# Last layer's feed-forward: GpSimd's scaling and adding given to VectorE and ScalarE, half of u's fp32 values by ScalarE, gates read a step apart

## The chip, the cores and the metric

One core of a Trainium2 chip runs the whole kernel. The metric is device time in microseconds (us); a kernel's number is the median of its runs. TensorE (PE) does matrix products and transposes, VectorE (DVE), ScalarE (ACT) and GpSimd (POOL) the elementwise work, and SyncE (SP) issues the transfers. Each engine runs its instructions in the order in which the program lists them.

## The reference

A backbone of two layers works on 256 latent and 256 context tokens of width 1024, batch 1. Layer 0 mixes by windowed attention, layer 1 (the last) by a state-space scan; each is followed by a feed-forward block of width 4096. Shifts, scales and gates (six vectors per layer) come from a small conditioning product with `w_mod`. What matters here, for the latent tokens `x` of the last layer:

```python
ALPHA = (2.0 * DEPTH) ** 0.25
def layer_norm(x, g, b):
    ...
    y = (xf - mu) * lax.rsqrt(var + LN_EPS) * g + b
def modulate(h, shift, scale):
    return h * (1.0 + scale) + shift
def squared_relu_mlp(h, w1, w2):
    return jnp.square(jax.nn.relu(h @ w1)) @ w2
```

The mixer's output, times its gate, is added to ALPHA times the stream and normalised (`mixg`, `mixb` are that norm's g and b). The result, modulated, goes through the feed-forward; the feed-forward's output, times its gate, is added to ALPHA times the same result and normalised again.

## The kernel before

All values are fp32. For TensorE each operand is split into a high part, rounded to fp32r, and a low part, the fp32 value less the high part; a product then takes three matmuls: high by high (L79), low by high (L80), high by low (L81). In the last layer the down-projections do the same on L261 to L263. PE is the busiest engine.

Weights stream from memory in 1 MB pieces named `raw` (`emit_w`, two buffers). ScalarE makes each high part `wh` (L61) and VectorE each low part `wl` (L62), 128x512 at a time. `next_w` hands out the next 1024 columns and emits pieces up to `ahead` further than the one asked for.

**Layer 0's feed-forward** runs in four rounds. In a round eight hidden blocks m0 to m7 are made (tile `f0a`): ScalarE does relu and square, VectorE squares again in fp32 (L357) and subtracts (L358), which gives the low part `f0fl`. Then eight output blocks (`f0b`) each need all eight hidden blocks, and VectorE adds each to the stream (L346). Between these steps the program draws single steps from a generator, `mods_sums`, that makes the last layer's modulation vectors. It loads eight 512 KB pieces `wm` (two buffers, so a piece is issued when the piece two before it has been used) and VectorE sums them, scaled, into `ma` (L140 the first, L142 the others, 128x1024 each). For the two gates (numbers 2 and 5) two matmuls on PE (L149) and two additions on VectorE (L150) follow, matmul and addition in the same step.

**The last layer's tail** works on rows: two tiles of 128 tokens, i = 0 and 1. For each tile the last part of the mixer's down-projection `so` ends on PE; the stream is transposed on PE and copied to `Xt` by ScalarE (L1021); VectorE multiplies by the gate, adds and takes statistics (L270 to L272, 128x512 each); L278 to L280 finish mean and deviation; L290 normalises the row tile in place. PE transposes it in 128x128 pieces (L296), two banks of four pieces. From each piece come

```python
nc.scalar.activation(uh[k][:, c], p, AF.Identity, bias=sh, scale=sc)
t = self.tmp.tile([128, 256], F32, tag="t1", name="ut")[:, :128]
nc.vector.tensor_scalar(t, p, sc, sh, op0=ALU.mult, op1=ALU.add)
nc.vector.tensor_sub(ul[k][:, c], t, uh[k][:, c].bitcast(F32))
```

which are L301 (`u4h`, ScalarE), L303 (`ut`, VectorE) and L304 (`u4l`, VectorE). The first four hidden blocks are made by rows: 24 matmuls per tile (`f1r`, L1034 to L1036), relu by ScalarE (L364, tile `rr`), square by VectorE (L365), four transposes on PE (L368), then high and low parts (L372, L373). From then on PE runs hidden blocks (`f1a`) and down-projections to the end.

The feed-forward's residual needs the normalised row tile times ALPHA g plus ALPHA b. GpSimd does that: `mixg` and `mixb` (128x1024, loaded by `row`) are scaled once (L1056), then each row tile is multiplied (L1058) and added to (L1059) in place, 128x1024 per instruction. The code stands behind round c = 0 of the last feed-forward; a scheduler places each instruction on its engine by priority and readiness, and GpSimd has nothing else to do by then.

Of the kernel before, what the change touches and what calls it, by code (L numbers as in the profile page):

```python
# [8 lines left out]
F32 = mybir.dt.float32  # L9
F32R = mybir.dt.float32r  # L10
BF16 = mybir.dt.bfloat16
AF = mybir.ActivationFunctionType
ALU = mybir.AluOpType
# [26 lines left out]
class Net:  # L40
# [90 lines left out]
    def mods_sums(self, i, b, streams, gate=None):  # L131
# [12 lines left out]
        if gate is not None:  # L144
            nc.sync.dma_start(gate, self.a["rows"][(2, 5).index(b), :].partition_broadcast(128))
            for h in range(2):
                c = slice(512 * h, 512 * h + 512)
                ps = self.bank("md", f"mod{i}{b}{h}")
                nc.tensor.matmul(ps, self.avg, acc[0][:, c], start=True, stop=True)  # L149
                nc.vector.scalar_tensor_tensor(gate[:, c], ps, 32.0 * 1024, gate[:, c], op0=ALU.mult, op1=ALU.add)  # L150
                yield
            return
# [133 lines left out]
    def ln_mid(self, i, x, st, aff, uh, ul):  # L286
# [5 lines left out]
        for q in range(2):  # L292
# [4 lines left out]
            for m in range(4):  # L297
                k = 4 * q + m
                p = pt[:, 128 * m:128 * m + 128]
                sc, sh = aff[:, 0, k:k + 1], aff[:, 1, k:k + 1]  # L300
                nc.scalar.activation(uh[k][:, c], p, AF.Identity, bias=sh, scale=sc)  # L301
                t = self.tmp.tile([128, 256], F32, tag="t1", name="ut")[:, :128]
                nc.vector.tensor_scalar(t, p, sc, sh, op0=ALU.mult, op1=ALU.add)  # L303
                nc.vector.tensor_sub(ul[k][:, c], t, uh[k][:, c].bitcast(F32))  # L304
# [666 lines left out]
    def layer1(self):  # L971
# [35 lines left out]
        with tc.tile_pool(name="tk", bufs=1) as self.tk, tc.tile_pool(name="fp1", bufs=2) as fp:  # L1007
            X = self.tk.tile([128, 2, 1024], F32, name="Xt")
            ws = [self.next_w(whole=True) for _ in range(4)]
            bn = [self.stat_tile(f"bm{i}") for i in range(2)]  # L1010
# [30 lines left out]
            for c in range(4):  # L1041
# [10 lines left out]
                for m in range(8 if c < 3 else 4):  # L1052
                    self.down(acc, lh(m), ll(m), self.next_w(whole=True), 8 * c + m, False)
                if c == 0:
                    for t in (ag, ab):
                        nc.gpsimd.tensor_scalar(t, t, ALPHA, 0.0, op0=ALU.mult, op1=ALU.add)  # L1056
                    for i in range(2):
                        nc.gpsimd.tensor_tensor(X[:, i, :], X[:, i, :], ag, op=ALU.mult)  # L1058
                        nc.gpsimd.tensor_tensor(X[:, i, :], X[:, i, :], ab, op=ALU.add)  # L1059
            ws = [self.next_w(whole=True) for _ in range(4)]  # L1060
# [106 lines left out]
```

## Time and profile before

| | us |
|---|---|
| runs of the kernel before | 1215.44, 1210.81, 1210.56 (median 1210.81) |
| the profiled execution | 1204.13 |
| its span | 1202.3 |
| PE busy | 1139.5 (95%) |
| VectorE busy | 845.2 (70%) |
| ScalarE busy | 600.7 (50%) |
| GpSimd busy | 62.7 (5%) |

The span runs from the first to the last instruction of the profiled execution; its granted TensorE clock was 0.984 of full speed on average. PE is busy nearly throughout, so the time is PE's work plus the few stretches in which PE waits or runs at the lower clock. The timelines list an engine's instructions by start, with the idle time ahead of one in brackets and what ended it; the chain of waits follows the end of the program back through what released each step.

### The profile page before, as it was taken

The page shows a single profiled execution, that of the slowest core. Times are in us where ns is not written, and L with a number is a line of the kernel's source. Part 1 is how long each engine was busy: PE and PEld are TensorE (multiplying, and loading weights), DVE is VectorE, ACT ScalarE, POOL GpSimd, SP SyncE. Part 2 cuts the span into 40 slices and gives each one's busy share as a digit, 9 for nine tenths or more (in the row PEclk, how much of TensorE's full clock was granted, in tenths as well). Part 3 has the DMA queues.
Part 4 walks back from the last instruction along what each step waited for, and adds up shares of the span by engine and source line. Part 5 has one row for each costly group of instructions (what it writes and reads, how often), then busy time and mean ns, then how long its engine had stood idle before and what let it go on. Part 6 is the DMA issues. An engine that isn't in the chain of part 4 may idle for free.

```text
span 1202.3 us, 18548 instructions
## 1 busy us (share of the span) xinstructions
PE 1139.5 (95%) x6976; PEld 916.9 (76%) x6976; DVE 845.2 (70%) x1701; ACT 600.7 (50%) x1372; POOL 62.7 (5%) x85
## 2 busy tenths in 40 slices
PE   5999999998999999989999898999999985999996
PEld 4766767887988878868898786777777674898995
DVE  4498677668958677744434889989898678565666
ACT  4376666235512322312323747787968654454551
POOL 1200000005000000000000500000000021000000
PEclk8999999999999999999999999999999997999999
DMA  8735331441645567633222125434544561555551
GB/s 327 296 109 172 110 125 48 136 145 38 206 144 179 167 215 277 222 131 105 93 82 72 44 108 160 141 116 166 171 144 143 215 220 47 188 185 180 197 186 70
DMA packets 41433, 182.79 MB, mean 152 GB/s; under 512 B 4608, under 2 KB 5248, under 8 KB 28288
## 3 DMA queue, kind: packets, MB, share of 16 engines
q1 hardware_dynamic: 41056, 181.36, 44.5%
q8 instruction: 55, 0.90, 0.3%
q10 hardware_dynamic: 288, 0.26, 0.1%
q14 instruction: 34, 0.28, 0.1%
HBM read 180.41 MB, written 1.18 MB: 151 GB/s over the span
## 4 chain that ended last, share of the span: by engine, by line
PE 77%; DVE 11%; DMA 5%; ACT 5%; issue 2%; DVEq 0%; SPq 0%; ACTq 0%
PE f0b L79 5%; PE f0b L81 5%; PE f0b L80 5%; PE f0a L79 5%; PE f0a L80 4%; PE f0a L81 4%; PE y L942 3%; PE o L503 2%; PE f L263 2%; PE f L262 2%; PE f1a L79 2%; PE f1a L81 2%; PE f1a L80 2%; PE f L261 2%; DMA wm<-in_w_mod 2%
## 5 line engine op out<-in xcount | busy, mean ns | idle before, releaser
L61 ACT CAST wh<-raw 128x512 fp32r<-128x512 f32 x404 | 237.4, 619 | 406.5 <-PE f0b L80 126.4
L62 DVE TENSOR_TENSOR wl<-raw,wh 128x512 fp32r<-128x512 f32 x404 | 268.9, 687 | 124.7 <-ACT wh L61 124.0
L80 PE MATMUL f0b<-f0fl,wh 128*128 128x512 f32 (+1 forms) x320 | 111.9, 350 | 3.5 <-DVE f0fl L358 3.5
L79 PE MATMUL f0b<-f0fh,wh 128*128 128x512 f32 (+1 forms) x320 | 114.6, 359 | 0.0
L79 PE MATMUL f0a<-u1h,wh 128*128 128x512 f32 (+1 forms) x320 | 111.4, 350 | 1.5 <-ACT u1h L181 1.5
L81 PE MATMUL f0b<-f0fh,wl 128*128 128x512 f32 (+1 forms) x320 | 112.3, 351 | 0.0
L81 PE MATMUL f0a<-u1h,wl 128*128 128x512 f32 (+1 forms) x320 | 110.9, 347 | 0.0
L80 PE MATMUL f0a<-u1l,wh 128*128 128x512 f32 (+1 forms) x320 | 110.9, 349 | 0.0
L142 DVE SCALAR_TENSOR_TENSOR ma<-wm,cs,ma 128x1024 f32<-128x1024 f32 x70 | 88.7, 1281 | 25.9 <-DMA wm<-in_w_mod 25.7
L80 PEld LDWEIGHTS f0b<-f0fl,wh 128*128 128x128 f32 x320 | 60.5, 189 | 13.6 <-DVE f0fl L358 4.2
L79 PEld LDWEIGHTS f0a<-u1h,wh 128*128 128x128 f32 x320 | 60.3, 189 | 11.7 <-ACT u1h L181 2.3
L81 PEld LDWEIGHTS f0b<-f0fh,wl 128*128 128x128 f32 x320 | 60.6, 189 | 10.5 <-issue 2.1
L79 PEld LDWEIGHTS f0b<-f0fh,wh 128*128 128x128 f32 x320 | 60.4, 189 | 10.6 <-issue 2.6
L81 PEld LDWEIGHTS f0a<-u1h,wl 128*128 128x128 f32 x320 | 60.6, 189 | 8.1 <-issue 0.4
L80 PEld LDWEIGHTS f0a<-u1l,wh 128*128 128x128 f32 x320 | 60.3, 189 | 7.8 <-issue 0.4
L79 PE MATMUL f1a<-u4h,wh 128*128 128x256 f32 x224 | 64.3, 287 | 0.0
L81 PE MATMUL f1a<-u4h,wl 128*128 128x256 f32 x224 | 64.1, 286 | 0.0
L80 PE MATMUL f1a<-u4l,wh 128*128 128x256 f32 x224 | 64.1, 286 | 0.0
L346 DVE SCALAR_TENSOR_TENSOR X<-f0b,mT,X 128x256 f32<-128x256 f32 x48 | 21.0, 479 | 47.2 <-PE f0b L81 47.2
L79 PE MATMUL x<-u2h,wh 128*128 128x512 f32 x128 | 51.3, 401 | 2.1 <-DVE cy L753 2.1
L926 ACT ACTIVATE W<-A,sT 128x128 f32<-128x128 f32 (+1 forms) x128 | 50.0, 458 | 3.8 <-PE y L942 2.5
L81 PE MATMUL x<-u2h,wl 128*128 128x512 f32 x128 | 51.0, 400 | 0.7 <-DVE wl L62 0.7
(438 smaller groups left out, 2760.1 us busy)
## 6 DMA issues: line engine op xcount, KB each, us to landing
raw<-in_wall SPq DMA_DIRECT2D x102, 1024.0 KB, 5.0
wm<-in_w_mod SPq DMA_DIRECT2D x96, 512.0 KB, 4.5
A<-dq SPq DMA_DIRECT2D x32, 256.0 KB, 4.7
E<-dq SPq DMA_DIRECT2D x32, 256.0 KB, 4.9
X<-in_xT SPq DMA_DIRECT2D x8, 256.0 KB, 8.4
gate<-in_rows SPq DMA_DIRECT2D x2, 512.0 KB, 12.3
out_dram<-Xt SPq DMA_DIRECT2D x4, 256.0 KB, 2.0
mixg<-in_rows SPq DMA_DIRECT2D x1, 512.0 KB, 6.1
```

Of the source, the lines that this page charges most:

```text
L61: nc.scalar.copy(h, src[:, c])
L62: nc.vector.tensor_sub(l, src[:, c], h.bitcast(F32))
L79: mm(ps, wh[:, k, :], ah[k][:, c0:c1], start=(k == 0), stop=False)
L80: mm(ps, wh[:, k, :], al[k][:, c0:c1], start=False, stop=False)
L81: mm(ps, wl[:, k, :], ah[k][:, c0:c1], start=False, stop=(k == 7))
L142: nc.vector.scalar_tensor_tensor(t, wm, c, t, op0=ALU.mult, op1=ALU.add)
L261: mm(ps, lh(i), wh[:, c], start=(k == 0), stop=False)
L262: mm(ps, ll(i), wh[:, c], start=False, stop=False)
L263: mm(ps, lh(i), wl[:, c], start=False, stop=last)
L503: nc.tensor.matmul(po[64 * a:64 * a + 64, :], self.V[:, kt, g * 64:g * 64 + 64], PT[a][:, i * n:i * n + n], start=(i == 0), stop=(i == len ...
L926: nc.scalar.activation(W[:, h, o:o + l1 - l0], A[:, h, l0:l1], AF.Relu, scale=-1.0, bias=self.sT[:, st, r + h:r + h + 1])
L942: mm(ps[64 * a:64 * a + 64, l0:l1], lh[:, hc:hc + 64], mv, start=(n == 0), stop=(n == 5))
```

## The change

Five edits. (1) The two scalings of `mixg` and `mixb` go from GpSimd to ScalarE. (2) The multiplication and addition on the row tiles go from GpSimd to VectorE, as eight instructions of 128x512 (L1066) in place of four of 128x1024, and the block of code is written behind round c = 1 instead of c = 0. (3) For odd pieces `ut` is computed by ScalarE (L306) instead of VectorE, and `ut` has four buffers of its own. (4) A gate's matmul and its addition are drawn in steps of their own, with one more empty step ahead. (5) The last four pieces of the mixer's down-projection are asked for with `ahead=0`.

```diff
--- before.py
+++ after.py
@@ -144,9 +144,11 @@
         if gate is not None:
             nc.sync.dma_start(gate, self.a["rows"][(2, 5).index(b), :].partition_broadcast(128))
             for h in range(2):
+                yield
                 c = slice(512 * h, 512 * h + 512)
                 ps = self.bank("md", f"mod{i}{b}{h}")
                 nc.tensor.matmul(ps, self.avg, acc[0][:, c], start=True, stop=True)
+                yield
                 nc.vector.scalar_tensor_tensor(gate[:, c], ps, 32.0 * 1024, gate[:, c], op0=ALU.mult, op1=ALU.add)
                 yield
             return
@@ -299,8 +301,11 @@
                 p = pt[:, 128 * m:128 * m + 128]
                 sc, sh = aff[:, 0, k:k + 1], aff[:, 1, k:k + 1]
                 nc.scalar.activation(uh[k][:, c], p, AF.Identity, bias=sh, scale=sc)
-                t = self.tmp.tile([128, 256], F32, tag="t1", name="ut")[:, :128]
-                nc.vector.tensor_scalar(t, p, sc, sh, op0=ALU.mult, op1=ALU.add)
+                t = self.tk.tile([128, 128], F32, tag="ut", name="ut", bufs=4)
+                if m % 2:
+                    nc.scalar.activation(t, p, AF.Identity, bias=sh, scale=sc)
+                else:
+                    nc.vector.tensor_scalar(t, p, sc, sh, op0=ALU.mult, op1=ALU.add)
                 nc.vector.tensor_sub(ul[k][:, c], t, uh[k][:, c].bitcast(F32))
 
     def ln_out(self, i, x, st, g, b):
@@ -1006,7 +1011,7 @@
         u4h, u4l = self.new_act("u4")
         with tc.tile_pool(name="tk", bufs=1) as self.tk, tc.tile_pool(name="fp1", bufs=2) as fp:
             X = self.tk.tile([128, 2, 1024], F32, name="Xt")
-            ws = [self.next_w(whole=True) for _ in range(4)]
+            ws = [self.next_w(whole=True, ahead=0) for _ in range(4)]
             bn = [self.stat_tile(f"bm{i}") for i in range(2)]
             for i in range(2):
                 for h in range(2):
@@ -1051,12 +1056,14 @@
                 ll = lambda m: (lambda i: fs[m][1][:, 128 * i:128 * i + 128])
                 for m in range(8 if c < 3 else 4):
                     self.down(acc, lh(m), ll(m), self.next_w(whole=True), 8 * c + m, False)
-                if c == 0:
+                if c == 1:
                     for t in (ag, ab):
-                        nc.gpsimd.tensor_scalar(t, t, ALPHA, 0.0, op0=ALU.mult, op1=ALU.add)
+                        nc.scalar.activation(t, t, AF.Copy, scale=ALPHA)
                     for i in range(2):
-                        nc.gpsimd.tensor_tensor(X[:, i, :], X[:, i, :], ag, op=ALU.mult)
-                        nc.gpsimd.tensor_tensor(X[:, i, :], X[:, i, :], ab, op=ALU.add)
+                        for t, op in ((ag, ALU.mult), (ab, ALU.add)):
+                            for h in range(2):
+                                x = X[:, i, 512 * h:512 * h + 512]
+                                nc.vector.tensor_tensor(x, x, t[:, 512 * h:512 * h + 512], op=op)
             ws = [self.next_w(whole=True) for _ in range(4)]
             bn = [self.stat_tile(f"bf{i}") for i in range(2)]
             for i in range(2):
```

The change also moves instructions. On VectorE in the third round of layer 0's feed-forward, up to the low part of hidden block m7 (the last `f0fl`; the one ahead of it is m6's), the kernel before has:

```order
L142 SCALAR_TENSOR_TENSOR ma_5080<-wm_5173,cs,ma_5080 128x1024
L62 TENSOR_TENSOR wl_5224<-raw_5221,wh_5223 128x512
L357 TENSOR_TENSOR q<-r 128x512
L142 SCALAR_TENSOR_TENSOR ma_5080<-wm_5215,cs,ma_5080 128x1024
L358 TENSOR_TENSOR f0fl_5138<-q,f0fh_5137 128x512
L62 TENSOR_TENSOR wl_5224<-raw_5221,wh_5223 128x512
L142 SCALAR_TENSOR_TENSOR ma_5080<-wm_5218,cs,ma_5080 128x1024
L357 TENSOR_TENSOR q<-r 128x512
L142 SCALAR_TENSOR_TENSOR ma_5080<-wm_5256,cs,ma_5080 128x1024
L358 TENSOR_TENSOR f0fl_5183<-q,f0fh_5182 128x512
```

and the changed kernel (L357 is now L362, L358 is L363):

```order
L362 TENSOR_TENSOR q<-r 128x512
L140 TENSOR_SCALAR ma_5160<-wm_5161,cs 128x1024
L363 TENSOR_TENSOR f0fl_5117<-q,f0fh_5116 128x512
L109 TENSOR_TENSOR mT_85<-mod_5149,vecs 128x8
L142 SCALAR_TENSOR_TENSOR ma_5160<-wm_5203,cs,ma_5160 128x1024
L114 TENSOR_SCALAR mT_85<-mT_85 128x8
L62 TENSOR_TENSOR wl_5212<-raw_5209,wh_5211 128x512
L142 SCALAR_TENSOR_TENSOR ma_5160<-wm_5206,cs,ma_5160 128x1024
L62 TENSOR_TENSOR wl_5251<-raw_5209,wh_5250 128x512
L362 TENSOR_TENSOR q<-r 128x512
L142 SCALAR_TENSOR_TENSOR ma_5160<-wm_5244,cs,ma_5160 128x1024
L363 TENSOR_TENSOR f0fl_5171<-q,f0fh_5170 128x512
```

Of the gate's eight pieces of `wm` the kernel before uses all ahead of m7's low part (seven L142 stand between the low parts of m4 and m7); the changed kernel uses four, `wm_5161` to `wm_5244` (four L142, the first for an earlier sum, and one L140 stand between m4 and m7), and the other four come behind it, among the additions of `f0b`. The gate's two matmuls on PE stand behind the fourth `f0b` block instead of the first.

On VectorE in the tail, from the normalisation of the second row tile (L290, now L292) on, the kernel before has:

```order
L290 TENSOR_SCALAR Xt<-Xt,lm11mv 128x1024
L304 TENSOR_TENSOR u4l_9582<-ut,u4h_9574 128x128
L303 TENSOR_SCALAR ut<-ut_9691,affm_9562 128x128
L62 TENSOR_TENSOR wl_9812<-raw_9803,wh_9811 128x512
L304 TENSOR_TENSOR u4l_9583<-ut,u4h_9575 128x128
L62 TENSOR_TENSOR wl_9812<-raw_9803,wh_9811 128x512
L303 TENSOR_SCALAR ut<-ut_9761,affm_9562 128x128
L304 TENSOR_TENSOR u4l_9576<-ut,u4h_9568 128x128
L303 TENSOR_SCALAR ut<-ut_9761,affm_9562 128x128
L304 TENSOR_TENSOR u4l_9577<-ut,u4h_9569 128x128
L303 TENSOR_SCALAR ut<-ut_9761,affm_9562 128x128
L304 TENSOR_TENSOR u4l_9578<-ut,u4h_9570 128x128
```

and the changed kernel (L303 is now L308 on VectorE, L304 is L309):

```order
L292 TENSOR_SCALAR Xt<-Xt,lm11mv 128x1024
L309 TENSOR_TENSOR u4l_9583<-ut,u4h_9575 128x128
L62 TENSOR_TENSOR wl_9812<-raw_9803,wh_9811 128x512 x2
L1066 TENSOR_TENSOR Xt<-Xt,mixg_9925 128x512
L308 TENSOR_SCALAR ut<-ut_9747,affm_9562 128x128
L1066 TENSOR_TENSOR Xt<-Xt,mixg_9925 128x512
L309 TENSOR_TENSOR u4l_9576<-ut,u4h_9568 128x128
L1066 TENSOR_TENSOR Xt<-Xt,mixb_9927 128x512
L309 TENSOR_TENSOR u4l_9577<-ut,u4h_9569 128x128
L308 TENSOR_SCALAR ut<-ut_9747,affm_9562 128x128
L1066 TENSOR_TENSOR Xt<-Xt,mixb_9927 128x512
L309 TENSOR_TENSOR u4l_9578<-ut,u4h_9570 128x128
```

All eight L1066 stand between this normalisation and the first `rr` (L365, now L370), mixed with the second tile's `ut` and `u4l`; four `ut` of eight are gone from this stretch, and four from the first tile's.

On ScalarE ahead of the mixer's last down-projection, where `yh` is the high part of the scan's output, the kernel before has:

```order
L61 CAST wh_9524<-raw_9522 128x512 x2
L959 CAST yh_6512<-X_80 128x256
L959 CAST yh_6513<-X_80 128x256
L959 CAST yh_6514<-X_80 128x256
L61 CAST wh_9542<-raw_9522 128x512 x2
L959 CAST yh_6515<-X_80 128x256
```

and the changed kernel:

```order
L61 CAST wh_9524<-raw_9522 128x512 x2
L1061 ACTIVATE mixg_9925<-mixg_9925 128x1024
L964 CAST yh_6512<-X_80 128x256
L964 CAST yh_6513<-X_80 128x256
L1061 ACTIVATE mixb_9927<-mixb_9927 128x1024
L964 CAST yh_6514<-X_80 128x256
L964 CAST yh_6515<-X_80 128x256
L61 CAST wh_9542<-raw_9522 128x512 x2
```

The two scalings stand among the `yh` casts; the two `wh` casts that stood ahead of the last of these now follow it.

## Rows read from the trace of the kernel before

**Rows 1.** Windows: PE, PEld, DVE, ACT, POOL busy (x), PEclk, DMA, GB/s

```profile
960.00:1020.00 60.00, 43.46 (x198) 35.07 (x197) 46.87 (x91) 28.04 (x59) 13.78 (x6) 0.89 0.39 139
```

**Rows 2.** Timeline of PE, tail: start, us, what ran, [idle before <-releaser]

```profile
1000.28 1.94 PE L296 MATMUL ut<-con,Xt 128*128 128x128 f32 x8 [11.83 <-DVE Xt L290]
...
1012.70 0.66 PE L368 MATMUL rt<-con,rr 128*128 128x128 f32 x4 [4.58 <-DVE rr L365]
...
1022.33 0.66 PE L368 MATMUL rt<-con,rr 128*128 128x128 f32 x4 [1.87 <-DVE rr L365]
...
1022.95 0.28 PE L80 MATMUL f1a<-u4l,wh 128*128 128x256 f32 x1
...
1024.17 0.41 PE L79 MATMUL f1a<-u4h,wh 128*128 128x256 f32 x1
```

**Rows 3.** Timeline of VectorE over the same tail, same columns

```profile
987.57 0.40 DVE L303 TENSOR_SCALAR ut<-ut,affm 128x128 f32<-128x128 f32 x1
987.89 2.53 DVE L271 TENSOR_TENSOR Xt<-Xt,gt 128x512 f32<-128x512 f32 x1
990.35 2.42 DVE L304 TENSOR_TENSOR u4l<-ut,u4h 128x128 fp32r<-128x128 f32 x1
992.69 0.68 DVE L272 BATCH_NORM_STATS2 bm<-Xt 128x6 f32<-128x512 f32 x1
...
994.20 0.28 DVE L304 TENSOR_TENSOR u4l<-ut,u4h 128x128 fp32r<-128x128 f32 x1
994.40 0.68 DVE L271 TENSOR_TENSOR Xt<-Xt,gt 128x512 f32<-128x512 f32 x1
995.00 0.40 DVE L303 TENSOR_SCALAR ut<-ut,affm 128x128 f32<-128x128 f32 x1
...
999.34 0.80 DVE L290 TENSOR_SCALAR Xt<-Xt,lm11mv 128x1024 f32<-128x1024 f32 x1
...
1002.42 2.43 DVE L304 TENSOR_TENSOR u4l<-ut,u4h 128x128 fp32r<-128x128 f32 x1
...
1005.21 2.12 DVE L304 TENSOR_TENSOR u4l<-ut,u4h 128x128 fp32r<-128x128 f32 x1
...
1011.96 0.69 DVE L365 TENSOR_TENSOR rr<-rr 128x512 f32<-128x512 f32 x1
```

**Rows 4.** Timeline of GpSimd over the same tail

```profile
989.95 2.67 POOL L1059 TENSOR_TENSOR Xt<-Xt,mixb 128x1024 f32<-128x1024 f32 x1
1002.31 2.39 POOL L1058 TENSOR_TENSOR Xt<-Xt,mixg 128x1024 f32<-128x1024 f32 x1 [9.69 <-PE ut L296]
```

**Rows 5.** Timeline of PE in layer 0's feed-forward

```profile
516.53 0.40 PE L79 MATMUL f0b<-f0fh,wh 128*128 128x512 f32 x1
520.39 0.50 PE L80 MATMUL f0b<-f0fl,wh 128*128 128x512 f32 x1 [3.46 <-DVE f0fl L358]
```

**Rows 6.** Timeline of VectorE in layer 0's feed-forward

```profile
496.96 0.75 DVE L140 TENSOR_SCALAR ma<-wm,cs 128x1024 f32<-128x1024 f32 x1
...
516.65 1.29 DVE L142 SCALAR_TENSOR_TENSOR ma<-wm,cs,ma 128x1024 f32<-128x1024 f32 x1 [3.20 <-DMA wm<-in_w_mod]
517.85 0.69 DVE L357 TENSOR_TENSOR q<-r 128x512 f32<-128x512 f32 x1
```

**Rows 7.** Chain of waits in layer 0's feed-forward: start, us, what

```profile
509.58 6.98 DMA wm<-in_w_mod
...
522.02 0.43 PE f0b L79
```

**Rows 8.** Timeline of ScalarE in layer 0's feed-forward

```profile
506.77 0.59 ACT L354 ACTIVATE r<-f0a 128x512 f32<-128x512 f32 x1
```

**Rows 9.** The page's DMA issues: KB each, median us to landing

```profile
wm<-in_w_mod SPq DMA_DIRECT2D x96, 512.0 KB, 4.5
```

**Rows 10.** Timeline of ScalarE before the last down-projection

```profile
971.69 1.14 ACT L61 CAST wh<-raw 128x512 fp32r<-128x512 f32 x2 [1.22 <-PE so L262]
974.42 1.14 ACT L61 CAST wh<-raw 128x512 fp32r<-128x512 f32 x2 [1.59 <-PE so L262]
```

## Prediction

> **What bounds the kernel now.** I read the page first: PE is busy 95% of a span of 1202.3 us, so a change to the other engines can only save where PE waits, or where it runs slowly after a wait. The windows of 60 us show one stretch that is far from full: from 960 to 1020, PE is busy 43.46 us and GpSimd works 13.78 us in six instructions, which are just the six that this change takes from it [rows 1]. In PE's timeline of that stretch the reader sees three waits, all for VectorE: 11.83 us for the second row tile's normalisation, 4.58 us and 1.87 us for `rr` [rows 2]. So in the tail VectorE is the limit. The same list for the windows around layer 0's feed-forward has a single wait, 3.46 us for m7's low part [rows 5].
>
> VectorE's timeline tells why the tail is slow. Four instructions are far longer than their like: L271 takes 2.46 us from its start to the next start, against 0.60 for the one at 994.40, and three L304 take 2.34, 2.35 and 2.04 where 0.20 is usual (994.20 to 994.40) [rows 3]; for the last two I take the duration less 0.08, the overlap with the neighbour that the first two show. GpSimd's timeline lies exactly over them: its addition of 989.95 ends at 992.62 and VectorE's next instruction starts at 992.69; its multiplication of 1002.31 ends at 1004.70, and the L304 that began at 1002.42 ends at 1004.85. Two rows of four GpSimd instructions are shown; the four pair off with the four long ones in this way [rows 3, 4]. What the pairs share: GpSimd reads two row-sized operands, VectorE reads two operands from SBUF. L303, whose data come from PSUM, is not lengthened.
>
> **The tail, part by part.** Prices are starts to next starts: 0.60 for a two-operand 128x512, 0.32 for a `ut` (987.57 to 987.89), 0.20 for a `u4l` [rows 3].
>
> *From 987.57 to the second normalisation at 999.34.* With GpSimd silent, L271 gives back 1.86 and the L304 2.14, 4.0 together. Of the `ut` in this stretch three go to ScalarE, 3 x 0.32 = 1.0, and one more `u4l` (0.20) stands ahead of the normalisation. That makes 4.8. ScalarE now does three more pieces, in turn with VectorE on one PSUM bank; I set 0.6 against that, since VectorE had no gap here to hide a wait in. Gain 4.2: the normalisation starts at 995.1.
>
> *From there to `rr`.* Before, 1011.96 - 999.34 = 12.6 us [rows 3]. In the changed order VectorE has, behind the start of the normalisation: itself 0.7, nine `u4l` 1.8, two `wl` at 1.2, four `ut` 1.3, and the eight L1066, 8 x 0.60 = 4.8. Sum 9.8. ScalarE's share of these pieces is twelve instructions, each at most half of the 1.14 us that two casts of 128x512 take [rows 10], under 7 us, so it lies beside. PE's 24 matmuls for the first tile end 4.58 ahead of 1012.70, at 1008.1 [rows 2], 8.8 after the normalisation, so they lie beside VectorE's 9.8 too. Gain 2.8, and 7.0 for the tail: `rr` at 1005.0. PE's 4.58 wait becomes about 1.8; late next is still `rr`, by VectorE's queue, and the eight additions are all ahead of it. Bounds: if all other waits stay as they are, the four long ones give 1.86 + 2.14 + 2.15 + 1.84 = 8.0, eight `ut` 2.6, and the additions take 4.8 back: 5.8. If the shorter wait of PE no longer brings the clock down, nine matmuls at 0.43 [rows 7] instead of 0.23 give 1.8 more: 8.8. I take the clock's fall as staying, because after the 1.87 us wait it fell as well: a matmul of f1a takes 0.41 at 1024.17 where 0.28 is normal [rows 2].
>
> The split of four additions into eight costs nothing by the rows: a 128x1024 sum takes 1.20 (516.65 to 517.85), twice the 0.60 of a 128x512 [rows 3, 6]. The Trainium skill, Perfetto Trace Analysis (section Optimizing Scalar/DVE Operations), speaks against it: each VectorE instruction on SBUF carries some 60 ns of its own, and larger ones are better where the engine is saturated. By it the split would cost 4 x 0.06 = 0.24 us, and the tail would give 6.8; no row here shows that overhead.
>
> *The scalings on ScalarE.* Two instructions of 128x1024, each as long as two casts, about 1.1, so 2.1 us [rows 10]. ScalarE waits for PE 1.22 and 1.59 us right behind them, 2.8 together, which hides them. If that cover were gone, 2.1 would fall on PE. `ahead=0`: the number of `wl` ahead of the second normalisation is unchanged in the order; nothing.
>
> **Layer 0's feed-forward.** PE did its last matmul without m7's low part at 516.53 and could have used it by 516.75; it started at 520.39 [rows 5]. Behind it the clock was at the lower of its two levels (1.2 instead of 2.4 GHz): a matmul of 512 columns came every 0.43 us [rows 7] instead of every 0.23 (516.53 to where the next one was due, 516.75), for nine of them: 1.75 us lost. So 5.2 us are there to be had. The cause: VectorE's queue has the seventh piece's sum ahead of m7's square, its transfer was issued at 509.58 and took 6.98 us, and then came L142, square, L142, low part, to 520.34 [rows 6, 7].
>
> In the changed order two sums fewer stand between the low parts of m4 and m7, so m6's square runs when its relu is done (506.77 + 0.59, [rows 8]) at 507.4, the square is done at 508.0, the first sum, an L140 of 0.75 at most [rows 6], at 508.7, m6's low part at 509.3, the second sum at 510.5. Then the fourth piece is issued, a buffer being free. What it takes decides. With the page's median, 4.5 us [rows 9], it lands at 515.1; one L142 (1.20) and one subtraction (0.7) later m7's low part is there, at 517.0 to 517.1, a wait of 0.3. With 6.98 it is 519.6, a wait of 2.9. I take the median, since the `raw` piece that shared the path with the slow one is issued in the changed order behind m5's square and lands before; 0.5 us of wait stay. Gain 3.5 + 1.75 - 0.5 = 4.7. Bounds: 0.6 (the transfer stays slow, the clock falls all the same) and 5.2. The gate's matmuls come three `f0b` blocks later, near 533, and the last of its eight sums near 528 by the same steps, so PE doesn't wait for them. Edit (4) adds nothing else.
>
> **The sum.** 7.0 + 4.7 = 11.7 us off the profiled execution, 1204.13 to 1192.4. That execution stands 6.7 us under the median of the runs shown, 1210.81; on the median the forecast is 1199.1. About 0.5%, 6 us, is what a measurement here can tell from no change, so faster means under 1204.8.
>
> **The rivals.**
> *The transfer stays slow.* The fourth piece is late as the seventh was, and only the tail gains: 7.0 + 0.6, 1203.2. For it: the piece is issued a microsecond later than before, 510.5 against 509.58. Against it: no 1 MB piece ahead of it. 0.20.
> *Both at the low ends.* VectorE waits in the tail as often as before, and the transfer is slow: 5.8 + 0.6 = 6.4, 1204.4, on the edge of what can be told. The alternation between VectorE and ScalarE on one bank speaks for it. 0.10.
> *The clock stays up* behind PE's shorter wait in the tail: 1197.3. 0.06.
> *The long VectorE instructions are not GpSimd's doing*, but that stretch's own traffic. Then L271 stays at 2.46, and the eight L1066, of its form and on the same `Xt`, take as long: 8 x 2.46 = 19.7, less 2.6 for `ut`, 17.1 on the path, less 4.7: 12.4 slower, 1223. It decides from 0.9 us per addition on (8 x 0.9 = 7.3 = 2.6 + 4.7). Against it: many L62, with two SBUF operands, run at 0.60 in the same stretch between GpSimd's instructions, and the long ones end with GpSimd's. The Trainium skill, SBUF — State Buffer (section Who interferes with whom), has the same: a VectorE instruction with two SBUF inputs contends with a GpSimd one that reads SBUF, and the one that began first holds the other off until it is done. By that rule the additions run freely once GpSimd is silent, and the trace's four pairs agree [rows 3, 4]. The chance, from the pairs alone, is 0.03.
>
> **How the numbers follow.** The forecast keeps 0.61. Its own bounds are 5.8 + 4.0 and 8.8 + 5.2, 1201 to 1196.8. The range also takes in the slow transfer (1203.2) and the low ends (1204.4), and a little for the difference between runs below, whose profiled one was 6.7 under the median: 1194 to 1205.5. Faster: the forecast, the clock case, 0.14 of the slow transfer (it lies 1.6 us from the bound) and half of the low ends, 0.86; same the rest of these, 0.11; slower 0.03.
>
> **What would show it.** Right: GpSimd idle from 960 on; no VectorE instruction of two SBUF operands above 1.3 us between 978 and 1010; the second normalisation some 4 us earlier against the first; eight L1066 at 0.60; PE's waits of 11.83 and 4.58 down to about 7.6 and 1.8; in the first part, the 3.46 us wait under 1 and no matmuls at 0.43 behind it. Wrong: L271 or L304 still above 2 us; L1066 above 0.9; PE waiting behind the `yh` casts for ScalarE; a wait for m7's low part or for `ma` of over 2 us.

## The result, and the profile after

The changed kernel took 1193.19 us (median of four runs, 1190.3 to 1194.7), the kernel before 1210.85. The medians differ by 17.7 us; the ratio of the two kernels is 0.9843 with a 95% interval of 0.9812 to 0.9873, or 19.0 us (15.4 to 22.8). It is faster, as forecast, but the forecast was 1199.1, 11.7 us faster, and 1193.2 lies 0.8 under the range. A second comparison of the same two kernels, with more runs of the kernel before (e7 below), gave 0.9869 (0.9849 to 0.9889), 15.8 us (13.4 to 18.2); that one is used from here on. One of the twelve runs of e1 took 1414.8 us at a mean granted clock of 0.747 and stands in no comparison below.

The profiled execution took 1194.7 us, span 1192.9. The windows, with the columns of [rows 1] (start:end, length, then PE, PEld, DVE, ACT, POOL busy with their instructions, PEclk, DMA share, GB/s), for layer 0's feed-forward, before and after, and for the tail after:

```profile
480.00:540.00 60.00, 56.54 (x243) 44.88 (x243) 37.81 (x56) 16.77 (x32) 0.94 (x3) 0.97 0.54 182
```

```profile
480.00:540.00 60.00, 60.00 (x274) 47.94 (x273) 44.52 (x64) 20.20 (x38) 0.93 (x3) 1.00 0.64 214
960.00:1020.00 60.00, 49.31 (x249) 40.64 (x249) 46.51 (x103) 36.33 (x80) 0.00 (x0) 0.94 0.51 176
```

PE is now busy all of the 60 us from 480 on, where it had 56.5. In the tail's window it gained 5.9 us of work, its granted clock stands at 0.94 instead of 0.89, and GpSimd has nothing. PE's timeline of the tail, to be compared with [rows 2]:

```profile
996.68 1.94 PE L298 MATMUL ut<-con,Xt 128*128 128x128 f32 x8 [7.33 <-DVE Xt L292]
...
1006.39 0.66 PE L373 MATMUL rt<-con,rr 128*128 128x128 f32 x4 [1.41 <-DVE rr L370]
...
1007.14 0.40 PE L1040 MATMUL f1r<-wh,u4l 128*128 128x512 f32 x1
1007.37 0.40 PE L1041 MATMUL f1r<-wl,u4h 128*128 128x512 f32 x1
...
1014.37 0.66 PE L373 MATMUL rt<-con,rr 128*128 128x128 f32 x4 [1.81 <-DVE rr L370]
...
1015.59 0.28 PE L79 MATMUL f1a<-u4h,wh 128*128 128x256 f32 x1
...
1026.39 0.40 PE L263 MATMUL f<-wh,f1fh 128*128 128x512 f32 x1
```

Before, the matmuls behind the second wait and the first of the down-projection were:

```profile
1013.53 0.63 PE L1035 MATMUL f1r<-wh,u4l 128*128 128x512 f32 x1
1013.96 0.63 PE L1036 MATMUL f1r<-wl,u4h 128*128 128x512 f32 x1
...
1035.82 0.39 PE L261 MATMUL f<-wh,f1fh 128*128 128x512 f32 x1
```

The waits of 11.83, 4.58 and 1.87 us are 7.33, 1.41 and 1.81. What stands behind them changed too: the matmuls of 512 columns behind the second wait start every 0.23 us, not every 0.43, and those of 256 columns behind the third take 0.28, not 0.41 [rows 2]. The granted clock says the same. Behind the second wait it is 0.55 before (1013.0 to 1016.8) and 1.00 after (1006.8 to 1012.0); behind the third it is 0.50 before (1023.6 to 1026.9) and 1.00 after (1014.8 to 1018.4). Behind the first, longest wait it is 0.50 in both. VectorE's timeline of the same stretch, to be compared with [rows 3]:

```profile
988.98 0.69 DVE L273 TENSOR_TENSOR Xt<-Xt,gt 128x512 f32<-128x512 f32 x1
989.62 0.29 DVE L309 TENSOR_TENSOR u4l<-ut,u4h 128x128 fp32r<-128x128 f32 x1
...
995.72 0.81 DVE L292 TENSOR_SCALAR Xt<-Xt,lm11mv 128x1024 f32<-128x1024 f32 x1
...
997.85 0.69 DVE L1066 TENSOR_TENSOR Xt<-Xt,mixg 128x512 f32<-128x512 f32 x1
998.45 0.41 DVE L308 TENSOR_SCALAR ut<-ut,affm 128x128 f32<-128x128 f32 x1
...
1004.76 0.68 DVE L1066 TENSOR_TENSOR Xt<-Xt,mixb 128x512 f32<-128x512 f32 x1
...
1005.65 0.69 DVE L370 TENSOR_TENSOR rr<-rr 128x512 f32<-128x512 f32 x1
```

L273 (L271 before) takes 0.69 and L309 (L304 before) 0.29, the additions 0.60 from start to start (997.85 to 998.45). VectorE's last `u4l` ends at 1005.64, and so does, at 1005.62, ScalarE's relu from which `rr` is made. From the second normalisation to `rr` it is 1005.65 - 995.72 = 9.9 us, against 12.6 before; the sum in the prediction was 9.8. ScalarE, ahead of the last down-projection (compare [rows 10]):

```profile
967.75 1.06 ACT L1061 ACTIVATE mixg<-mixg 128x1024 f32<-128x1024 f32 x1
...
972.61 1.14 ACT L61 CAST wh<-raw 128x512 fp32r<-128x512 f32 x2 [0.60 <-PE so L264]
975.34 1.14 ACT L61 CAST wh<-raw 128x512 fp32r<-128x512 f32 x2 [1.59 <-PE so L264]
```

The scalings take 1.06 each. ScalarE's waits for PE there, 1.22 and 1.59 before, are 0.60 and 1.59 now: the cover held. The first row tile's normalisation comes 63.3 us after the tail's first `so` matmul, 63.4 before, so nothing there is later for it. In layer 0's feed-forward, PE's timeline (compare [rows 5]) and VectorE's (compare [rows 6]):

```profile
520.38 0.39 PE L79 MATMUL f0b<-f0fh,wh 128*128 128x512 f32 x1
520.61 0.39 PE L80 MATMUL f0b<-f0fl,wh 128*128 128x512 f32 x1
```

```profile
515.89 1.29 DVE L142 SCALAR_TENSOR_TENSOR ma<-wm,cs,ma 128x1024 f32<-128x1024 f32 x1 [1.70 <-DMA wm<-in_w_mod]
...
517.70 0.68 DVE L362 TENSOR_TENSOR q<-r 128x512 f32<-128x512 f32 x1
518.30 1.28 DVE L142 SCALAR_TENSOR_TENSOR ma<-wm,cs,ma 128x1024 f32<-128x1024 f32 x1
519.49 0.68 DVE L363 TENSOR_TENSOR f0fl<-q,f0fh 128x512 fp32r<-128x512 f32 x1
```

The second row of PE's is the matmul that waited 3.46 us before. It starts without a gap; m7's low part (L363) was done at 520.2, 0.4 us ahead of it. A transfer is still waited for, 1.70 us, but for the third piece's sum; the fourth piece is there when VectorE comes to it.

### The profile page after: what moved, and what is told of

The parts are those of the page before. It is cut to its first block, busy times and chain, and to the rows that moved or that the text cites. A ratio compares the mean times of both kernels' runs of the same rounds, so it can differ in the third digit from the quotient of the medians.

```text
span 1192.9 us, 18539 instructions
## 1 busy us (share of the span) xinstructions
PE 1140.3 (96%) x6976; PEld 917.5 (77%) x6976; DVE 839.5 (70%) x1701; ACT 604.3 (51%) x1382; POOL 48.1 (4%) x79
## 4 chain that ended last, share of the span: by engine, by line
PE 79%; DVE 8%; DMA 5%; ACT 5%; issue 1%; DVEq 0%; SPq 0%; ACTq 0%
PE f0a L79 5%; PE f0a L80 5%; PE f0a L81 5%; PE f0b L79 5%; PE f0b L81 5%; PE f0b L80 5%; PE y L947 3%; PE o L508 2%; PE f L265 2%; PE f L264 2%; PE f L263 2%; PE f1a L81 2%; PE f1a L79 2%; PE f1a L80 2%; DMA raw<-in_wall 2%; PE x L81 2%
## 5 line engine op out<-in xcount | busy, mean ns | idle before, releaser
L62 DVE TENSOR_TENSOR wl<-raw,wh 128x512 fp32r<-128x512 f32 x404 | 268.4, 686 | 129.3 <-ACT wh L61 128.4
L142 DVE SCALAR_TENSOR_TENSOR ma<-wm,cs,ma 128x1024 f32<-128x1024 f32 x70 | 88.7, 1280 | 17.8 <-DMA wm<-in_w_mod 17.7
L81 PEld LDWEIGHTS f0b<-f0fh,wl 128*128 128x128 f32 x320 | 60.1, 188 | 10.4 <-issue 2.1
L79 PEld LDWEIGHTS f0b<-f0fh,wh 128*128 128x128 f32 x320 | 60.1, 188 | 10.4 <-issue 2.6
L80 PE MATMUL f1a<-u4l,wh 128*128 128x256 f32 x224 | 63.4, 283 | 0.0
```

The source lines that it names most:

```text
L62: nc.vector.tensor_sub(l, src[:, c], h.bitcast(F32))
L79: mm(ps, wh[:, k, :], ah[k][:, c0:c1], start=(k == 0), stop=False)
L80: mm(ps, wh[:, k, :], al[k][:, c0:c1], start=False, stop=False)
L81: mm(ps, wl[:, k, :], ah[k][:, c0:c1], start=False, stop=(k == 7))
L142: nc.vector.scalar_tensor_tensor(t, wm, c, t, op0=ALU.mult, op1=ALU.add)
```

## The experiments

Two durations were read from PE's timeline in each trace, so that stretches which an edit doesn't touch stay out of the comparison. **Feed-forward**: from the first output block of layer 0's first round to the first hidden block of its fourth. **Tail**: from the first `so` matmul of the scan to the first down-projection of the last feed-forward. "Timed" is the ratio to the kernel before measured beside it, as us of its median; a minus is slower.

| kernel | feed-forward | tail | timed, us faster (interval) |
|---|---|---|---|
| before | 233.7 | 114.8 | |
| e1 before, again | 236.5 | 115.6 | -1.2 (-3.6 to 1.2) |
| after | 228.1 | 104.4 | 19.0 (15.4 to 22.8) |
| e7 after, again | 228.9 | 104.7 | 15.8 (13.4 to 18.2) |
| e3 gates only | 228.2 | 114.5 | 6.5 (4.5 to 8.5) |
| e4 all but the gates | 234.2 | 104.6 | 9.1 (6.8 to 11.2) |
| e6 GpSimd's work left out | 232.2 | 105.1 | 10.5 (8.2 to 12.8) |
| e2 GpSimd's work moved, nothing else | 233.9 | 108.9 | 8.6 (5.8 to 11.2) |
| e5 ut split only | 235.7 | 112.5 | 1.8 (-0.1 to 3.9) |
| e8 all but GpSimd's work | 228.1 | 112.6 | 9.1 (5.9 to 12.1) |
| e9 all but `ahead=0` | 228.1 | 104.7 | 16.6 (12.5 to 20.8) |
| e10 additions of 128x1024 | 228.2 | 104.8 | 17.2 (12.2 to 22.0) |
| e11 rows' transposes later | 228.2 | 101.4 | 20.3 (18.0 to 22.5) |
| e12 and first row tile earlier | 228.2 | 102.1 | 19.8 (17.8 to 22.0) |

**e1, the kernel before again.** No edit.

> The kernel before, unchanged, run against itself. Theory: its executions differ by several us (the profiled one shown was 1204.1, the runs 1210.6 to 1215.4), so the ratio is 1.000 within 0.005, and a new trace shows the same three waits of PE in the tail (11.8, 4.6, 1.9 us) and the one of 3.5 us in layer 0's feed-forward, while stretches that no edit touches move by a few us. Rival: the executions agree within 0.3%, and the 7 us between the profiled one and the median are a matter of the profile alone.

The ratio is 1.001 (0.999 to 1.003); the 17 executions of the same kernel beside it lie between 1204.7 and 1214.1 us. So the executions differ by several us, and the profiled one before (1204.13) was quicker than all of these. The list of PE's waits from 420 to 540 (line waited for: total us, times, longest) shows where part of that comes from:

```profile
PE f0b L80 <- DVE f0fl L358: 4.8, 1, 4.8
PE mod L149 <- DVE ma L142: 1.1, 1, 1.1
```

The same program order waits 4.8 us here for m7's low part, not 3.5, and 1.1 us for a gate's sum (L149), of which the first trace had nothing.

**e3, the gates alone.**

```diff
             for h in range(2):
+                yield
                 ...
                 nc.tensor.matmul(ps, self.avg, acc[0][:, c], start=True, stop=True)
+                yield
```

> Only edit (4), the gates read a step apart. Theory: PE's wait for m7's low part (3.5 us) and the low clock behind it (1.75 us) go, 5.2 us faster; the tail keeps its waits of 11.8, 4.6 and 1.9. Rival, the transfer stays slow: a wait of 2 to 3 us for m7's low part is left and the time moves by under 1 us.

From 420 to 540 PE has no wait left. The tail keeps its own (PE's waits, same columns; `rr` has two, the longer is 3.5):

```profile
PE ut L298 <- DVE Xt L292: 11.8, 1, 11.8
PE rt L370 <- DVE rr L367: 5.3, 2, 3.5
```

Timed, it is 6.5 us faster (4.5 to 8.5). The theory holds; the rival, a transfer that stays slow, falls: the fourth piece took 4.5 us here, and 4.5 to 4.7 in all eight traces with the new order.

**e4, the changed kernel without the gates' edit.**

```diff
             for h in range(2):
-                yield
                 ...
                 nc.tensor.matmul(ps, self.avg, acc[0][:, c], start=True, stop=True)
-                yield
```

> The changed kernel without edit (4). Theory: the tail gains as in the whole change, 7.0 us by VectorE's queue and some 3 by the clock that no longer falls behind PE's shorter waits, about 10 us faster than before; the wait of 3.5 us for m7's low part is back. Rival, the clock is no part of it: 7 us.

```profile
PE ut L296 <- DVE Xt L290: 7.3, 1, 7.3
PE f0b L80 <- DVE f0fl L361: 3.8, 1, 3.8
PE rt L371 <- DVE rr L368: 3.2, 2, 1.8
```

The tail's waits are those of the changed kernel, the wait for m7's low part is back at 3.8 us, and the tail is 10.2 us shorter than in the trace before. Timed, 9.1 (6.8 to 11.2) leaves both the theory's 10 and the rival's 7 open, but the trace decides: from the transposes behind the second wait to those behind the third it takes 8.0 us, as in the changed kernel, and not 9.6 as before. So the clock is part of it. 9.1 and e3's 6.5 make 15.6; e7 measured 15.8 for both.

**e6, GpSimd silent.**

```diff
-                if c == 0:
-                    for t in (ag, ab):
-                        nc.gpsimd.tensor_scalar(t, t, ALPHA, 0.0, op0=ALU.mult, op1=ALU.add)
-                    for i in range(2):
-                        nc.gpsimd.tensor_tensor(X[:, i, :], X[:, i, :], ag, op=ALU.mult)
-                        nc.gpsimd.tensor_tensor(X[:, i, :], X[:, i, :], ab, op=ALU.add)
```

> The kernel before with GpSimd's six instructions left out, so that ALPHA g and ALPHA b of the last norm are not applied to the residual. Theory: the four long VectorE instructions (L271 2.5, L304 2.4, 2.4, 2.1 us) come to 0.7 and 0.3, the second normalisation stands 4.0 us earlier against the first, and the first rr 8.0 us earlier; PE's wait of 4.6 us comes to about 0.5. Rival, that stretch's own traffic makes them long: they stay above 2 us, and the time is the same.

All sixteen L304 (duration in ns, least, median, longest):

```profile
L304 DVE TENSOR_TENSOR u4l<-ut,u4h x16: 274/282/293, 992.0 to 1008.0; 128x128 fp32r<-128x128 f32 x16
```

and VectorE's and PE's timelines:

```profile
987.93 0.80 DVE L290 TENSOR_SCALAR Xt<-Xt,lm10mv 128x1024 f32<-128x1024 f32 x1
...
998.83 0.80 DVE L290 TENSOR_SCALAR Xt<-Xt,lm11mv 128x1024 f32<-128x1024 f32 x1
...
1008.95 0.69 DVE L365 TENSOR_TENSOR rr<-rr 128x512 f32<-128x512 f32 x1 [0.61 <-ACT rr L364]
```

```profile
1009.70 0.66 PE L368 MATMUL rt<-con,rr 128*128 128x128 f32 x4 [1.41 <-DVE rr L365]
...
1017.68 0.66 PE L368 MATMUL rt<-con,rr 128*128 128x128 f32 x4 [1.87 <-DVE rr L365]
...
1018.89 0.28 PE L79 MATMUL f1a<-u4h,wh 128*128 128x256 f32 x1
```

None of the long instructions is left. The second normalisation follows the first by 10.9 us instead of 14.9 (984.44 to 999.34 before), the 4.0 us expected. `rr` comes 10.1 us after it instead of 12.6: 6.5 us earlier in all, not 8.0, because VectorE is ahead by then: it waited 0.61 us for ScalarE's relu of the 24 matmuls. PE's wait of 1.41 us is then the chain from PE's last matmul through ScalarE's relu and VectorE's square back to PE; it stands at 1.41 or 1.42 in six traces, whatever VectorE had to do beside it. The clock stays at the higher level behind both waits for `rr`, though the second of them is 1.87 us, as long as in the kernel before, where the clock fell. So GpSimd's instructions had lengthened VectorE's, and without them, with nothing put in their place, the tail is 9.7 us shorter.

**e7, the changed kernel again.** No edit.

> The changed kernel, unchanged, timed again. Theory: its two parts add up, the 6.5 us of the gates alone and the 9.1 us of the rest, 15.6 us faster than before, ratio 0.987; the first comparison's 17.7 us is this sum and scatter. Rival: the parts help each other, and it stays at 19 us (ratio 0.984).

PE's waits in the tail are 7.34, 1.41 and 1.81 us, as in the first trace. In the feed-forward 0.5 us of the wait for m7's low part is left: the third piece took 5.2 us there, 4.1 in the first trace.

The time is 15.8 us shorter (13.4 to 18.2), as the parts add up. The first comparison's 19.0 comes from few runs, and the two intervals overlap.

**e2, GpSimd's work moved, and nothing else.** On the kernel before:

```diff
-                if c == 0:
+                if c == 1:
                     for t in (ag, ab):
-                        nc.gpsimd.tensor_scalar(t, t, ALPHA, 0.0, op0=ALU.mult, op1=ALU.add)
+                        nc.scalar.activation(t, t, AF.Copy, scale=ALPHA)
                     ...
+                                nc.vector.tensor_tensor(x, x, t[:, 512 * h:512 * h + 512], op=op)
```

> Only edits (1) and (2): the scalings to ScalarE, the additions to VectorE; ut stays on VectorE. Theory: the four long instructions are gone; the second normalisation 4.0 us earlier against the first; behind it VectorE has four ut more (1.3 us), but two of the additions stand behind rr: 9.9 us to rr, as in the whole change. So tail gain 6.7 us by the queue plus the clock, 8 to 10 us. Rival: GpSimd's silence is paid back by the eight additions (4.8 us), and only 4 us are left.

```profile
1011.26 0.92 PE L368 MATMUL rt<-con,rr 128*128 128x128 f32 x4 [2.08 <-DVE rr L365]
...
1020.88 0.66 PE L368 MATMUL rt<-con,rr 128*128 128x128 f32 x4 [1.87 <-DVE rr L365]
```

and VectorE's:

```profile
1010.52 0.68 DVE L365 TENSOR_TENSOR rr<-rr 128x512 f32<-128x512 f32 x1
...
1011.33 1.28 DVE L1061 TENSOR_TENSOR Xt<-Xt,mixb 128x512 f32<-128x512 f32 x2
```

The tail is 5.9 us shorter; the timed 8.6 has a wide interval. PE's second wait is 2.08, not 1.41. Two of the eight additions do stand behind `rr`, as expected (the last row is both), but the other six and all of the `ut` stand ahead of it, and `rr` starts 10.7 us after the normalisation (999.83), where the theory had 9.9. And behind both waits the clock is down as before the change: 9.6 us from the second to the third of these rows, as in the trace before (1012.70 to 1022.33), against 8.0 in the changed kernel and in e6. The first `rr` transposes come 85.8 us after the first `so` instead of 91.7, 5.9 earlier where the theory had 6.7. That is all of the tail's gain, between the theory's 8 to 10 and the rival's 4: the clock gave nothing here.

**e5, the `ut` split alone.** On the kernel before:

```diff
-                t = self.tmp.tile([128, 256], F32, tag="t1", name="ut")[:, :128]
-                nc.vector.tensor_scalar(t, p, sc, sh, op0=ALU.mult, op1=ALU.add)
+                t = self.tk.tile([128, 128], F32, tag="ut", name="ut", bufs=4)
+                if m % 2:
+                    nc.scalar.activation(t, p, AF.Identity, bias=sh, scale=sc)
+                else:
+                    nc.vector.tensor_scalar(t, p, sc, sh, op0=ALU.mult, op1=ALU.add)
```

> Only edit (3): half of ut by ScalarE, GpSimd at work as before. Theory: the long instructions stay above 2 us; eight ut at 0.32 leave VectorE, at most 2.6 us; 1 to 2.6 us faster. Rival: the alternation of VectorE and ScalarE on one bank is what held the tail, and this edit alone gives 4 us or more.

```profile
995.48 2.53 DVE L271 TENSOR_TENSOR Xt<-Xt,gt 128x512 f32<-128x512 f32 x1
997.94 2.42 DVE L307 TENSOR_TENSOR u4l<-ut,u4h 128x128 fp32r<-128x128 f32 x1
...
1009.18 2.69 DVE L307 TENSOR_TENSOR u4l<-ut,u4h 128x128 fp32r<-128x128 f32 x2
...
1012.23 2.06 DVE L307 TENSOR_TENSOR u4l<-ut,u4h 128x128 fp32r<-128x128 f32 x1
```

The four long ones are all there (the third row is two instructions, 2.69 together). The tail is 2.3 us shorter, within the theory's bounds: the first `rr` transposes come 1.9 us earlier, and 0.4 is left of what the clock cost behind one wait and gave back behind the other. Timed alone the edit can't be told from nothing (-0.1 to 3.9).

**e8, the changed kernel with GpSimd at its old work.**

```diff
-                if c == 1:
+                if c == 0:
                     for t in (ag, ab):
-                        nc.scalar.activation(t, t, AF.Copy, scale=ALPHA)
+                        nc.gpsimd.tensor_scalar(t, t, ALPHA, 0.0, op0=ALU.mult, op1=ALU.add)
                     for i in range(2):
-                        ...
+                        nc.gpsimd.tensor_tensor(X[:, i, :], X[:, i, :], ag, op=ALU.mult)
+                        nc.gpsimd.tensor_tensor(X[:, i, :], X[:, i, :], ab, op=ALU.add)
```

> The changed kernel with the scalings and additions left on GpSimd, four of 128x1024, in their old place. Theory: the lengthened VectorE instructions are back (four above 2 us, 8 us together), and only the gates (some 6.5 us) and the ut split (2.3 us) are left: about 8 us faster than before, 7 to 8 slower than the changed kernel. Rival: with ut split the long ones fall beside other work, and it is as fast as the changed kernel.

VectorE's timeline and GpSimd's:

```profile
985.52 2.54 DVE L62 TENSOR_TENSOR wl<-raw,wh 128x512 fp32r<-128x512 f32 x1
987.98 2.43 DVE L309 TENSOR_TENSOR u4l<-ut,u4h 128x128 fp32r<-128x128 f32 x1
```

```profile
984.78 2.73 POOL L1063 TENSOR_TENSOR Xt<-Xt,mixg 128x1024 f32<-128x1024 f32 x1 [18.76 <-DVE wl L62]
```

The first GpSimd instruction falls on another VectorE one here, a `wl` (L62), and that takes 2.54 instead of some 0.68. So it is not L271 or the `u4l` that are slow: in these traces it is whichever VectorE instruction with two operands in SBUF meets one of GpSimd's. The tail is 112.6, 8.2 us longer than in the changed kernel.

**e9, without `ahead=0`.**

```diff
-            ws = [self.next_w(whole=True, ahead=0) for _ in range(4)]
+            ws = [self.next_w(whole=True) for _ in range(4)]
```

> The changed kernel without edit (5), the last down-projection's pieces asked for with the usual look-ahead. Theory: nothing, within 1 us of the changed kernel. Rival: the weights of the first row blocks crowd VectorE's queue ahead of the second normalisation, 1 to 3 us slower than the changed kernel.

The tail is 104.7 against 104.4 and 104.7 in the two traces of the changed kernel: nothing can be seen of this edit.

**e10, four additions of 128x1024.**

```diff
-                        for t, op in ((ag, ALU.mult), (ab, ALU.add)):
-                            for h in range(2):
-                                x = X[:, i, 512 * h:512 * h + 512]
-                                nc.vector.tensor_tensor(x, x, t[:, 512 * h:512 * h + 512], op=op)
+                        for t, op in ((ag, ALU.mult), (ab, ALU.add)):
+                            x = X[:, i, :]
+                            nc.vector.tensor_tensor(x, x, t, op=op)
```

> The changed kernel with the additions as four instructions of 128x1024 instead of eight of 128x512. Theory, by the rows: 1.2 us each, the same 4.8 us in all, no change. Rival, by the overhead of each instruction that the Trainium skill states (Perfetto Trace Analysis, Optimizing Scalar/DVE Operations): 0.24 us faster, which is under what can be told by timing, but shows in the starts of VectorE's instructions.

```profile
993.69 1.22 DVE L1065 TENSOR_TENSOR Xt<-Xt,mixg 128x1024 f32<-128x1024 f32 x1
994.82 0.40 DVE L308 TENSOR_SCALAR ut<-ut,affm 128x128 f32<-128x128 f32 x1
```

A whole row takes 1.13 from start to start, two halves 1.20, so four save 0.28 us. The estimate from the Trainium skill's 60 ns for each VectorE instruction on SBUF (Perfetto Trace Analysis, Optimizing Scalar/DVE Operations) was 0.24; the trace agrees, with 0.07 for each instruction. The prediction's 1.20, taken from L142, was slightly high. In the tail nothing of it is seen (104.8): PE's second wait is 1.41 again.

**e11, the transposes of `rr` moved behind other matmuls.**

```diff
+            rows = []
             for i in range(2):
                 ...
-                self.hidden_rows(i, ps, first)
+                rows.append(ps)
+            self.hidden_rows(0, rows[0], first)
             ...
                     self.gemm(ps, w, u4h, u4l, 0, 256)
+                    if c == 0 and m == 4:
+                        self.hidden_rows(1, rows[1], first)
```

> The changed kernel with the transposes of each row tile's rr moved on PE: the first behind the second tile's 24 matmuls, the second behind the first f1a block. What is left of PE's waits for rr (1.41 and 1.81 us) is PE's own chain through ScalarE and VectorE, so other matmuls put into it hide both: 3.2 us faster than the changed kernel. Rival: the weights of the first f1a block come too late, and PE waits there instead for as long.

PE's waits from 975 to 1040, all of them:

```profile
PE ut L298 <- DVE Xt L292: 7.3, 1, 7.3
```

Both waits for `rr` are gone, the tail is 3.0 us shorter than the changed kernel's, and the ratio is 0.9832 (0.9814 to 0.9851): 1189.35 us, where the changed kernel beside it had 1193.13. It is faster than both kernels, and the rival falls: PE waits for no weights here.

**e12, the first row tile's matmuls ahead of the second's transposes.** On top of e11, the loop over 24 matmuls becomes a function `f1r(i)`, and the weights are asked for ahead of it:

```diff
+                if i == 1:
+                    ws = [self.next_w(whole=True) for _ in range(4)]
+                    rows = [f1r(0)]
                 self.ln_mid(i, X[:, i, :], bn[i], aff, u4h, u4l)
             ...
+            rows.append(f1r(1))
             self.hidden_rows(0, rows[0], first)
```

> The kernel of e11_rows_late with the first row tile's 24 matmuls put on PE ahead of the second tile's transposes, into the wait of 7.3 us for the second normalisation. Theory: 24 matmuls at 0.23 are 5.5 us; PE waits some 2 to 3 us longer for the second tile's pieces instead, since VectorE's and ScalarE's queue for them takes 10 us from the normalisation on; 2 to 4 us faster than e11_rows_late, ratio to before about 0.980. Rival: VectorE alone sets the end of the second tile, and it is the same as e11_rows_late (0.983).

```profile
PE f1r L1022 <- DVE u4l L309: 1.8, 2, 1.0
PE ut L298 <- DVE Xt L292: 1.6, 1, 1.6
PE f1r L1021 <- ACT Xt L1036: 1.1, 1, 1.1
```

The wait for the normalisation shrinks to 1.6 us, but PE waits for the second tile's pieces instead, and the matmuls of 512 columns behind the wait start every 0.43 us. The tail is 102.1 against 101.4, the ratio 0.9836: the rival's size. But the edit also moved work on VectorE: two more `wl` and two additions stand ahead of the second normalisation, which starts 13.0 us after the first (983.88 to 996.89) instead of 10.4 in e11. So VectorE's queue took back what PE won; what the move on PE alone is worth is not shown.

## Why the prediction was right in kind and short in size

*What bounds the tail.* Right. The four long instructions were GpSimd's doing: they are gone when it is silent (e6), stay when only the rest is changed (e5, e8), and hit another instruction when the order shifts (e8). The rival that laid them to the stretch's own traffic falls.

*Step one, 4.2 us to the second normalisation, and step two, 2.8 us to `rr`.* Right: PE's waits of 11.83 and 4.58 came to 7.33 and 1.41, 4.5 and 3.2 less, and `rr` started 9.9 us after the normalisation (9.8 in the sum). The first `rr` transposes come 84.4 us after the tail's first `so` matmul instead of 91.7, 7.3 earlier, where the sum had 7.0. It had PE's second wait at about 1.8; at 1.41 it meets the chain through ScalarE, which the sum didn't have as a floor. That cost nothing here, since ScalarE's relu and VectorE's queue ended within 0.02 us of each other.

*"I take the clock's fall as staying, because after the 1.87 us wait it fell as well."* This step failed, and it is the largest part of the miss. From the transposes behind the second wait to those behind the third it took 8.0 us after and 9.6 before, 1.65 less; from there to the first down-projection 12.0 and 13.5, 1.47 less: 3.1 us, at a granted clock of 1.00 behind both waits. The case "the clock stays up" stood in the text with 1.8 us and a chance of 0.06. It had only the first of the two stretches, and the row that it was judged by, 1.87, followed a wait of 4.58 with a stretch at the low level behind it; in the changed kernel a wait of 1.81 follows one of 1.41, and nothing falls. It is not the 0.06 us between 1.81 and 1.87: in e6 a wait of 1.87 follows one of 1.41, and nothing falls either. So a wait of the same length can have a slow stretch behind it or none, and one row could not settle it. What decides it stays open (see the last section).

*Layer 0's feed-forward, 4.7 us.* The mechanism was right, the size short. The wait is gone in all eight traces with the new order but e7's, where 0.5 us of it is left. The choice of the median transfer was right, too: the fourth piece took 4.6 us in the changed kernel, where the sum had 4.5. In the profiled execution itself the stretch took 233.7 us, against 228.25 on average over the eight, so 5.5 us were there to be had: the sum's 4.7, the 0.5 us of wait that it left but that isn't there, and 0.3 more. The rest comes from taking the price from one execution. In six traces with the old order PE waits 2.1 to 4.8 us for m7's low part, 3.5 on average, as in the profiled one; but five of them wait 0.3 to 1.5 us more for other sums (e1: 1.1 for L149; e6: 1.5 for L156), where the profiled one had nothing. The stretch takes 234.36 us on average over these six, 6.1 more than over the eight, and timed alone the edit gave 6.5.

*ScalarE's scalings, `ahead=0`, the split of the additions.* Nothing on the path, as priced: the first normalisation is no later (63.3 us after the first `so` matmul, 63.4 before), and e9 and e10 leave the tail as it is. The split did cost VectorE 0.28 us, where the rows had nothing.

*The sum.* 7.0 + 4.7 becomes 7.3 + 3.1 + 6.1 = 16.5, where 15.8 (13.4 to 18.2) was measured. Of the 4.8 us between the two sums 3.1 are the clock. The forecast was built against the profiled execution and put on the median as it stood; that holds only if this execution has the waits of the others, and in layer 0's feed-forward it lacked 0.6 us of them.

*What GpSimd's silence is worth, and what the rest of the edit pays.* In the trace, silence alone shortens the tail by 9.7 us (e6), the move alone by 5.9 (e2), the `ut` split alone by 2.3 (e5), and both by 10.2 (e4). The additions on VectorE are not free by themselves; the split makes room for them, and with it PE's second wait comes down to 1.41 us, and the clock stays up. That goes with it in the traces, and is why 5.9 and 2.3 don't add up to 10.2; that the shorter wait is the reason was not tested by itself.

## What to carry to other kernels

Look at GpSimd's timeline beside VectorE's wherever a VectorE instruction takes several times its usual length: a small amount of GpSimd work on two operands can hold the engine that is on the path, and moving it there can be cheaper than leaving it. Price the waits that hang on transfers from several executions, not from the one profiled. When a wait of TensorE shrinks, add up the slow stretches behind it, and behind the next wait too, as a term of its own.

## What was not expected of the hardware

The clock behind a wait does not go by the length of that wait alone. Behind a second wait of 1.41 us PE stayed at the higher level in each of the six traces that have it (after, e4, e6, e7, e9 with 1.42, e10); behind 2.08 (e2), 3.1 (e5, e8), 3.5 (e3), 4.2 (e1) and 4.58 (before) it ran its 512-column matmuls at 0.43 us. The third wait, 1.81 to 1.87 us, was followed by the low level in before, e1, e2 and e3, not in the others, though e6 has the same 1.87 us as before, e1 and e2, and e5 and e8 had a longer second wait than e2. No run was made to tell these apart.

The two engines hold each other off, they don't share. In e8 a `wl` began 0.74 us after GpSimd's first multiplication and ended 0.55 us after its end, so most of its work was done once GpSimd was through. In the other direction, GpSimd's first multiplication before began beside a row of four `wl`, which ran at their usual 0.60, and took 3.32 us against 2.39 later. The Trainium skill, SBUF — State Buffer (Who interferes with whom), says that the pair of ports which VectorE and GpSimd share is an exclusive lock, and that the order of issue decides which of the two is held off. The traces agree, with 8.0 us more on VectorE for 10.8 us of GpSimd's work.

Executions of one program on one core differ by up to 9.4 us here (1204.7 to 1214.1 for the kernel before, beside e1); of the 6.2 us between the spans of the two traces of that kernel, 2.8 lie in the feed-forward stretch, with its waits for transfers, and 0.85 in the tail.
